# The up projection of an MLP by seven half-width products for each pair of blocks

## The chip, the cores and the metric

The kernel runs on one core of a Trainium2 chip. Its time is device microseconds of one execution; before the change the median of three runs is 988.55 us (988.21 to 988.84). The profile comes from one further execution.

## The reference

One decoder block on 512 tokens of 1,024 channels, in float32: a mixer (a state-space scan beside a pooling branch, merged by gates) and an MLP, each behind a normalisation with a scale and a shift from a conditioning vector. The change touches the MLP:

```python
h = rmsnorm(x, norm_mlp_w[i]) * (1.0 + scale_f) + shift_f
x = x + gate_f * (jnp.square(jax.nn.relu(h @ w_up[i])) @ w_down[i])
return rmsnorm(x, norm_final_w)
```

w_up is 1024 x 4096 and w_down 4096 x 1024.

## The kernel before

Channels lie on the 128 partitions, tokens along the free dimension. A weight matrix is cut into units: 128 output channels by 1,024 inputs, eight blocks of 128 x 128, one transfer of 512 KB (`load_unit`, from L125). Every float32 operand is split into a rounded high part and a low part: ScalarE writes the high part of a unit (L131), VectorE subtracts it for the low part (L132). A product of a block is three matmuls, high x high, high x low, low x high (`mm3`, L141 to L143), so a unit is 24 matmuls of 512 tokens into one PSUM bank. L111 and L112 split activations in the same way.

Raw units pass through four RAW buffers, split ones through four pairs of HL buffers, activations through 50 S buffers; `Slots` hands them out in turn, and a user waits for the last reader of the one before. A scheduler orders the instructions at build time within each engine's own queue, by the order in which the program is written and by priority; on the chip each queue runs in that order.

Behind the mixer comes `wout`: five whole units, then the last three in two halves of 256 tokens (`HALVES`), so that the norm of the first half runs beside the second. For each half, `residual` (L685, with the square L692 and its sum L693) makes x1, `norm` sums the squares on TensorE (L164), takes root and reciprocal (L176, L177) and spreads the result (L180), and `modulate` (L187 to L189) makes h2, the split input of the MLP.

The MLP runs in four quarters of the 4,096 hidden channels. A quarter has eight `up` units (Relu from PSUM, L739, square on VectorE, L731, split) and eight down units on the quarter's eight hidden tiles `us`, each added to x1 by `residual` (L685). The first three up units (`up_first`, Relu at L753) and the last three down units run in halves. The last quarter adds the sums of squares of the final norm, which ends in L781 and the writing of the output.

Of the kernel before, what the change touches and what calls it, by code (L numbers as in the profile page):

```python
# [18 lines left out]
HG = 8  # L19
# [14 lines left out]


NSLOT, NRAW, NHL, NPU = 50, 4, 8, 3
H = T // 2
# [21 lines left out]
def block_kernel(tc, xT, crow, arow, par, adaT, wstart, wz, wx, wpool_in, wgate, wpw, wbs, wbp, wout, wup, wdn, out):  # L59
    nc = tc.nc  # L60
    act, dve, pool, pe, sp = nc.scalar, nc.vector, nc.gpsimd, nc.tensor, nc.sync

    with (
# [3 lines left out]
    ):  # L67
        count = [0]

        def slots(name, n, shape=(P, T), where=sb):  # L70
            def make(i, dt):
                count[0] += 1
                return where.tile(list(shape), dt, tag=f"{name}{i}", name=f"{name}{i}_{count[0]}", bufs=1)
# [4 lines left out]
        MT = slots("mt", 3, (P, HG, P))  # L78
        RAW = slots("raw", NRAW, (P, 1024))
        HL = slots("hl", NHL, (P, 1024))  # L80
        SM = slots("sm", 4, (P, NC))
        SM.put(*[SM.get() for _ in range(4)])
        PU, PS = slots("ps", 8, (P, T), psp), slots("ps", 8, (P, T), psp)
        PU.free, PS.free = PU.free[:NPU], PS.free[NPU:]

        par_t = sb.tile([P, NPAR], F32, name="par_t")
# [5 lines left out]
        cbc = sb.tile([P, DM], F32, name="cbc")  # L92
# [15 lines left out]
        def split(src):  # L108

            hi, lo = S.get(F32R), S.get(F32R)  # L110
            act.copy(hi, src)  # L111
            dve.tensor_tensor(lo, src, hi.bitcast(F32), ALU.subtract)  # L112
            return hi, lo

        def free(pairs):
            for hi, lo in pairs:
                S.put(hi, lo)
# [3 lines left out]
        def load_unit(src, n=1024, low=None, at=None, cols=1024):  # L121

            at = at or HL
            with tc.high_priority() if urgent[0] else nullcontext():
                r = RAW.get()  # L125
                sp.dma_start(r[:, :n], src)
                blocks, kept = [], []
                for a in range(0, n, cols):
                    w = min(cols, n - a)
                    hi, lo = at.get(F32R), at.get(F32R)  # L130
                    act.copy(hi[:, :w], r[:, a:a + w])  # L131
                    (low or dve).tensor_tensor(lo[:, :w], r[:, a:a + w], hi[:, :w].bitcast(F32), ALU.subtract)  # L132
                    blocks += [(hi[:, o:o + P], lo[:, o:o + P]) for o in range(0, w, P)]
                    kept += [hi, lo]
            RAW.put(r)
            at.put(*kept)
            return blocks

        def mm3(ps, w, x, start, stop, t0=0, t1=T):
            (whi, wlo), (xhi, xlo) = w, x  # L140
            pe.matmul(ps, whi, xhi[:, t0:t1], start=start, stop=False)  # L141
            pe.matmul(ps, whi, xlo[:, t0:t1], start=False, stop=False)  # L142
            pe.matmul(ps, wlo, xhi[:, t0:t1], start=False, stop=stop)  # L143
# [29 lines left out]
        def rstd(sums, n, c0, c1):  # L173
# [6 lines left out]
                pe.matmul(bc[:, c * P:(c + 1) * P], r[:, c:c + 1].broadcast_to([P, P]), ident, start=True, stop=True)  # L180
            SM.put(r)
            return bc

        def modulate(x, R, scale, shift, hi, lo, t0=0, t1=T):

            t = S.get()
            dve.scalar_tensor_tensor(t[:, t0:t1], x[:, t0:t1], scale, R[:, t0:t1], ALU.mult, ALU.mult)  # L187
            act.activation(hi[:, t0:t1], t[:, t0:t1], AF.Identity, bias=shift)
            dve.scalar_tensor_tensor(  # L189
                lo[:, t0:t1], t[:, t0:t1], shift, hi[:, t0:t1].bitcast(F32), ALU.add, ALU.subtract)  # L190
            S.put(t)


        dve.memset(ones, 1.0)
# [15 lines left out]
        with tc.manual_schedule():  # L210
# [24 lines left out]
            ps = PU.get()  # L235
# [446 lines left out]
        def residual(ps, j, gate, t0=0, t1=T, sums=True, apart=None):  # L682

            x = x1[j][:, t0:t1]
            dve.scalar_tensor_tensor(x, ps[:, t0:t1], mod[:, gate + j:gate + j + 1], x, ALU.mult, ALU.add)  # L685
            if not sums:
                return
            if j == 0 or apart is not None:
                act.activation((ssum if apart is None else apart)[:, t0:t1], x, AF.Square)
            else:  # L690
                s = F.get()
                act.activation(s[:, t0:t1], x, AF.Square)  # L692
                dve.tensor_tensor(ssum[:, t0:t1], ssum[:, t0:t1], s[:, t0:t1], ALU.add)  # L693
                F.put(s)

        def norm(t0, t1, sqs):
            c0, c1 = t0 // P, t1 // P
            ps = PU.get()
            column_sums(ps, sqs, c0, c1)
            bc = rstd(ps, DM, c0, c1)  # L700
            PU.put(ps)
            return bc
# [8 lines left out]
                amod[:, 8 + k:9 + k], mod[:, 32 + k:33 + k], 1.0, col("nmlp", k), ALU.add, ALU.mult)  # L711
        w = [load_unit(wout[j], at=S, cols=T) for j in (5, 6, 7)]
        h2 = [(S.get(F32R), S.get(F32R)) for _ in range(8)]
        for t0, t1 in HALVES:
            for j in (5, 6, 7):
                ps = PU.get()
                for k in range(8):
                    mm3(ps[:, t0:t1], w[j - 5][k], mg[k], k == 0, k == 7, t0, t1)
                residual(ps, j, 16, t0, t1)
                PU.put(ps)  # L720
            R = norm(t0, t1, [ssum])
            for k in range(8):
                modulate(x1[k], R, amod[:, 8 + k:9 + k], mod[:, 24 + k:25 + k], *h2[k], t0, t1)
            PU.put(R)
        free(mg)
        for j in range(45, 48):
            ada(j)


        def squared(u):  # L730
            dve.tensor_tensor(u, u, u, ALU.mult)  # L731
            p = split(u)
            F.put(u)
            return p

        def up(i):
            ps = unit(wup[i], h2)
            u = F.get()
            act.activation(u, ps, AF.Relu)  # L739
            PU.put(ps)  # L740
            return squared(u)

        def up_first():

            w = [load_unit(wup[i]) for i in range(3)]
            u = [F.get() for _ in range(3)]
            for t0, t1 in HALVES:
                ps = [PU.get() for _ in range(3)]
                for k in range(8):
                    for i in range(3):  # L750
                        mm3(ps[i][:, t0:t1], w[i][k], h2[k], k == 0, k == 7, t0, t1)
                for i in range(3):
                    act.activation(u[i][:, t0:t1], ps[i][:, t0:t1], AF.Relu)  # L753
                PU.put(*ps)
            return [squared(t) for t in u]

        for q in range(4):
            us = up_first() if q == 0 else []
            us += [up(8 * q + i) for i in range(len(us), 8)]
            for j in range(8 if q < 3 else 5):  # L760
                ps = unit(wdn[4 * j + q], us)
                residual(ps, j, 40, sums=q == 3)
                PU.put(ps)
                if q == 3:
                    act.activation(x1[j], x1[j], AF.Copy, scale=col("nfin", j))
            if q < 3:
                free(us)
        w = [load_unit(wdn[4 * j + 3]) for j in (5, 6, 7)]
        last_sq = F.get()
        for t0, t1 in HALVES:  # L770
            for j in (5, 6, 7):
                ps = PU.get()
                for k in range(8):
                    mm3(ps[:, t0:t1], w[j - 5][k], us[k], k == 0, k == 7, t0, t1)
                residual(ps, j, 40, t0, t1, apart=last_sq if j == 7 else None)
                act.activation(x1[j][:, t0:t1], x1[j][:, t0:t1], AF.Copy, scale=col("nfin", j))
                PU.put(ps)
            R = norm(t0, t1, [ssum, last_sq])
            for j0, j1 in ((0, 2), (2, 4), (4, 6), (6, 8)):
                x = xbig[j0 // 4][:, j0 % 4:j0 % 4 + j1 - j0, t0:t1]  # L780
                dve.tensor_tensor(x, x, R[:, t0:t1].unsqueeze(1).broadcast_to([P, j1 - j0, t1 - t0]), ALU.mult)  # L781
                sp.dma_start(out[j0:j1, :, t0:t1].rearrange("j p t -> p j t"), x)
            PU.put(R)


# [69 lines left out]
```

## Time and profile before

| | us |
|---|---|
| median of three runs | 988.55 |
| the profiled execution | 988.34 |
| its span, first to last instruction | 986.6 |
| TensorE's clock granted in it, mean share of full speed | 0.997 |

A row of a group names line, engine, operation, tiles and shape, how often it ran, its busy us in total and the mean ns of one, and behind the second bar the idle time of its engine just before it with what ended it. In a timeline the first two numbers are the start in the span and the duration, both in us. PE is TensorE, PEld its weight loads, DVE is VectorE, ACT ScalarE, POOL GpSimd, SP the queue of ordinary transfers.

### The profile page before, as it was taken

The numbers are of one execution on the slowest core, as the hardware profiler recorded it, in microseconds if no ns is written. First come the engines' busy times: TensorE is split into PE (matmuls) and PEld (weight loads), VectorE is DVE, ScalarE is ACT, GpSimd is POOL, SyncE is SP. The second block draws the span as 40 slices with busy tenths as digits, with TensorE's granted clock in tenths as the row PEclk, the third lists the DMA queues.
The fourth block names the chain that finished last, engine by engine and source line by source line (L and its number), as shares of the span: only waits on it lengthen the run. The fifth ranks groups of instructions, "written<-read, shape, count | busy, mean of one in ns | idle before, by whom it ended". The sixth has DMA issues, their size and how long they took to land.

```text
span 986.6 us, 12153 instructions
## 1 busy us (share of the span) xinstructions
PE 971.5 (98%) x4722; PEld 802.3 (81%) x4722; DVE 616.0 (62%) x882; ACT 482.1 (49%) x719; POOL 63.8 (6%) x71
## 2 busy tenths in 40 slices
PE   8999999999999999999999999999999999999997
PEld 6777777888878878788888888988888888888886
DVE  6996967676776776878775665654344334434443
ACT  5488997579558833563312343452233123313342
POOL 0101120120012013200000000000000000000000
PEclk9999999999999999999999999999999999999998
DMA  9747342443343233337885443032232323232302
GB/s 349 278 131 205 106 139 89 125 119 108 103 134 115 86 124 112 123 112 237 269 273 186 166 147 129 2 128 91 101 97 96 106 87 107 86 107 86 107 1 86
DMA packets 58620, 129.55 MB, mean 131 GB/s; under 512 B 4609, under 2 KB 29313, under 8 KB 58562
## 3 DMA queue, kind: packets, MB, share of 16 engines
q1 hardware_dynamic: 58562, 128.77, 40.0%
q8 instruction: 37, 0.61, 0.3%
q14 instruction: 21, 0.17, 0.1%
HBM read 126.53 MB, written 2.23 MB: 130 GB/s over the span
## 4 chain that ended last, share of the span: by engine, by line
PE 82%; DVE 6%; ACT 5%; issue 4%; DMA 1%; POOL 1%; SPq 0%; DVEq 0%; POOLq 0%; ACTq 0%
PE ps L141 26%; PE ps L142 26%; PE ps L143 26%; PE ps L492 1%; DMA mt<-cs_d 1%; ACT hl L131 1%; DVE sz L157 1%; DVE hl L252 1%; ACT L359 1%; ACT mt L444 1%; ACT L444 1%; POOL pad L560 1%; PE ps L476 1%; PE ps L472 1%; DVE xs L157 1%
## 5 line engine op out<-in xcount | busy, mean ns | idle before, releaser
L141 PE MATMUL ps<-s,hl 128*128 128x512 f32 (+1 forms) x1272 | 490.3, 386 | 2.0 <-ACT pad L551 1.5
L142 PE MATMUL ps<-s,hl 128*128 128x512 f32 (+1 forms) x1272 | 485.7, 382 | 0.7 <-DVE s L112 0.7
L143 PE MATMUL ps<-s,hl 128*128 128x512 f32 (+1 forms) x1272 | 485.2, 382 | 0.0
L131 ACT CAST hl<-raw 128x1024 fp32r<-128x1024 f32 x153 | 160.0, 1048 | 287.9 <-PE ps L142 272.9
L141 PEld LDWEIGHTS ps<-s,hl 128*128 128x128 f32 x1272 | 239.2, 188 | 52.0 <-issue 3.5
L142 PEld LDWEIGHTS ps<-s,hl 128*128 128x128 f32 x1272 | 239.4, 188 | 47.1 <-DVE s L112 1.6
L143 PEld LDWEIGHTS ps<-s,hl 128*128 128x128 f32 x1272 | 239.2, 188 | 46.1
L132 DVE TENSOR_TENSOR hl<-raw,hl 128x1024 fp32r<-128x1024 f32 x153 | 188.3, 1233 | 126.7 <-ACT hl L131 123.6
L685 DVE SCALAR_TENSOR_TENSOR xs<-ps,mod,xs 128x512 f32<-128x512 f32 (+1 forms) x46 | 31.3, 681 | 106.3 <-PE ps L143 106.1
L111 ACT CAST s<-sz 128x512 fp32r<-128x512 f32 x52 | 31.6, 620 | 52.9 <-DVE sz L731 42.3
L157 DVE CUSTOM_DVE_ANT_0 raw<-raw,cbc,par_t 128x1024 f32<-128x1024 f32 x32 | 40.9, 1278 | 18.6 <-DMA raw<-adaT 18.3
L112 DVE TENSOR_TENSOR s<-sz,s 128x512 fp32r<-128x512 f32 x52 | 35.1, 689 | 22.7 <-ACT s L111 22.7
L444 ACT ACTIVATE mt<-mt,ncs 128x128 f32<-128x128 f32 x128 | 41.5, 392 | 13.6 <-POOL mt L440 13.4
L355 DVE SCALAR_TENSOR_TENSOR s<-ps,par_t,s 128x511 f32<-128x511 f32 (+2 forms) x54 | 40.2, 744 | 3.2 <-ACT s L353 2.8
L289 PE MATMUL ps<-s,hl 128*128 128x512 f32 x144 | 35.8, 399 | 0.7 <-ACT s L277 0.6
L289 PEld LDWEIGHTS ps<-s,hl 128*128 128x128 f32 x144 | 26.3, 188 | 8.9 <-ACT s L277 3.3
L359 ACT ACT_TABLE_LOAD x20 | 25.7, 1283 | 8.1 <-DVE s L355 7.8
L515 POOL TENSOR_TENSOR s<-s 128x256 f32<-128x256 f32 x16 | 17.2, 1073 | 154.1 <-ACT s L514 154.0
L440 POOL TENSOR_SCALAR_AFFINE_SELECT mt<-mt 128x1024 f32<-128x1024 f32 x16 | 19.1, 1191 | 121.4 <-ACT cd L437 81.3
L444 ACT ACT_TABLE_LOAD x19 | 24.4, 1283 | 0.3
L445 DVE TENSOR_TENSOR mt<-mt,ps 128x1024 f32<-128x1024 f32 x16 | 19.5, 1217 | 7.2 <-PE ps L427 3.6
L111 ACT CAST s<-s 128x512 fp32r<-128x512 f32 x16 | 9.9, 621 | 25.0 <-DVE s L564 24.7
(160 smaller groups left out, 760.8 us busy)
## 6 DMA issues: line engine op xcount, KB each, us to landing
raw<-adaT SPq DMA_DIRECT2D x32, 512.0 KB, 4.1
raw<-wup SPq DMA_DIRECT2D x32, 512.0 KB, 3.3
raw<-wdn SPq DMA_DIRECT2D x32, 512.0 KB, 3.2
raw<-wx SPq DMA_DIRECT2D x18, 512.0 KB, 3.7
raw<-wz SPq DMA_DIRECT2D x16, 512.0 KB, 3.3
mt<-cs_d SPq DMA_DIRECT2D x16, 512.0 KB, 5.9
raw<-wbs SPq DMA_DIRECT2D x16, 512.0 KB, 3.4
raw<-wgate SPq DMA_DIRECT2D x16, 512.0 KB, 4.0
```

The lines of the kernel that those rows point to most:

```text
L111: act.copy(hi, src)
L112: dve.tensor_tensor(lo, src, hi.bitcast(F32), ALU.subtract)
L131: act.copy(hi[:, :w], r[:, a:a + w])
L132: (low or dve).tensor_tensor(lo[:, :w], r[:, a:a + w], hi[:, :w].bitcast(F32), ALU.subtract)
L141: pe.matmul(ps, whi, xhi[:, t0:t1], start=start, stop=False)
L142: pe.matmul(ps, whi, xlo[:, t0:t1], start=False, stop=False)
L143: pe.matmul(ps, wlo, xhi[:, t0:t1], start=False, stop=stop)
L157: dve.tensor_tensor_reduce(r, r, cbc, 1.0, col("b_ada", j), ALU.mult, ALU.add, mod[:, j:j + 1])
L289: pe.matmul(first[u], w[u][i // 2], h[k][i % 2], start=k == 0 and i == 0, stop=k == 7 and i == 2)
L355: dve.scalar_tensor_tensor(t[:, sh:], ps[:, :T - sh], w(3 - sh), t[:, sh:], ALU.mult, ALU.add)
L359: act.activation(o, t, AF.Silu)
L444: act.activation(m[:, i, :], m[:, i, :], AF.Exp, bias=ncs[:, c, g * HG + i:g * HG + i + 1])
```

## The change

Two neighbouring up units are a pair. Its weights, a 2 x 2 arrangement of blocks (two groups of output channels A11, A12 and so on by even and odd input blocks), and its input, two token halves by even and odd blocks (B11 to B22), are multiplied in seven products of half the width instead of eight: `product` is 4 input blocks x 3 matmuls x 256 tokens, 12 matmuls. Both sides need sums. Of the input there are four, T1 to T4, made once behind the second norm (`sums`) from the unsplit tiles `hf`, which are kept for that. Of each pair's weights there are four, S1 to S4: two are begun by transfers on GpSimd's queue that add to what lies in the buffer, the rest VectorE adds (`prepare`).

The first two pairs of units run plainly as `up_first`, now four units in halves, since the sums aren't ready. The other 14 pairs are `Pair` jobs. A pair collects its result in two banks of a `duo` (c11, c12) and one bank `ac`; ScalarE copies one product to s5 and one to c11 between, and VectorE adds ac and s5. The Relu then reads both halves from two banks, and the square moves to ScalarE (`activated`). `run_jobs` writes the products of neighbouring pairs in turns. The down units stay plain, the first two of a quarter interleaved.

Around that: RAW, HL and the tiles of the scan share one set `d` of 16 buffers, which in the MLP becomes 8 raw and 10 split buffers, with four more of half size; two raw buffers lie in the `sz` tile that held the sums of squares until the second norm. The pooling branch has three pad buffers instead of six. Weights are laid out by `pairs`. The scratch for descriptors of GpSimd's transfers goes back to its default size.

```diff
+        duo = [psp.tile([P, 2, T], F32, name=f"duo{i}") for i in range(2)]
...
-        PADS = slots("pad", 6, (P, T + 16))
+        PADS = slots("pad", 3, (P, T + 16))
...
+        def sums(u1, u2, t1, t2):
+
+            dve.tensor_tensor(u1[:, :H], u1[:, :H], u1[:, H:], ALU.subtract)
+            dve.tensor_tensor(u1[:, H:], u2[:, H:], u1[:, H:], ALU.subtract)
+            dve.scalar_tensor_tensor(u2[:, H:], u2[:, H:], -1.0, u1[:, :H], ALU.mult, ALU.subtract)
+            dve.scalar_tensor_tensor(u2[:, :H], u2[:, H:], -1.0, u2[:, :H], ALU.mult, ALU.subtract)
+            two(u1, t1)
+            two(u2, t2)
...
+            with tc.high_priority():
+                y1, y2, y3, y4 = RAW.get(), RAW.get(), RAW.get(), Y4.get()
+                sp.dma_start(y1, w[:, :1024])
+                sp.dma_start(y3[:, T:], w[:, :T])
+                pool.dma_start(y1[:, :T], w[:, 3 * T:], accum_op=ALU.add)
+                pool.dma_start(y3[:, T:], w[:, T:2 * T], accum_op=ALU.add)
+                sp.dma_start(y2[:, T:], w[:, 2 * T:3 * T])
+                sp.dma_start(y4, w[:, 3 * T:])
+                s1, a11 = parts(y1)
+                dve.tensor_tensor(y2[:, :T], y1[:, :T], y1[:, T:], ALU.add)
+                RAW.put(y1)
+                s2, a12 = parts(y2)
+                dve.tensor_tensor(y3[:, :T], y2[:, :T], y2[:, T:], ALU.add)
...
+        def product(ps, a, b, start=False):
+            for m in range(4):
+                w = tuple(x[:, m * P:(m + 1) * P] for x in a)
+                for i, (x, y) in enumerate(((w[0], b[m][0]), (w[0], b[m][1]), (w[1], b[m][0]))):
+                    pe.matmul(ps, x, y, start=start and m == 0 and i == 0, stop=m == 3 and i == 2, skip_group_check=True)
...
+            def open(self):
+                self.be, self.s5 = BE.get(), U5.get()
+                self.c11, self.c12 = self.be[:, 0, :H], self.be[:, 1, :H]
+                product(self.c12, self.a["S1"], self.b["T1"], True)
+                act.copy(self.s5, self.c12)
+
+            def first(self):
+                self.ac = AC.get()
+                product(self.ac[:, :H], self.a["A11"], self.b["B11"], True)
+                act.copy(self.c11, self.ac[:, :H])
+
+            def middle(self):
+                product(self.ac[:, :H], self.a["S2"], self.b["T2"])
+                dve.tensor_tensor(self.c12, self.ac[:, :H], self.s5, ALU.add)
+                product(self.c11, self.a["A12"], self.b["B21"])
+
+            def third(self):
+                product(self.ac[:, :H], self.a["S3"], self.b["T3"])
+                dve.tensor_tensor(self.ac[:, H:], self.ac[:, :H], self.s5, ALU.add)
+                U5.put(self.s5)
+
+            def close(self):
+                product(self.c12, self.a["S4"], self.b["B22"])
+                self.done(0, self.be[:, :, :H], 1)
+                BE.put(self.be)
+                product(self.ac[:, :H], self.a["A22"], self.b["T4"])
+                self.done(1, self.ac.rearrange("p (a b) -> p a b", a=2), -1)
+                AC.put(self.ac)
...
+        def activated(q, p, i, ps, sign):
+
+            u = U.get()
+            act.activation(ab(u), ps, AF.Relu, scale=float(sign))
+            act.activation(u, u, AF.Square)
+            two(u, us[2 * p + i])
+            U.put(u)
...
+        def up_first(w):
+
+            ps = [PU.get(), PU.get(), AC.get(), AC.get()]
+            for t0, t1 in HALVES:
+                for k in range(8):
+                    for i in range(4):
+                        mm3(ps[i][:, t0:t1], w[i][k], h2[k], k == 0, k == 7, t0, t1)
+            for k in range(8):
+                act.activation(hf[k], hf[k], AF.Identity, bias=mod[:, 24 + k:25 + k])
+            for m in range(4):
+                sums(*hf[2 * m:2 * m + 2], *h2t[m])
...
+            for b in duo:
+                pe.matmul(b[:, 0, :], h2[0][0][:, :P], h2[0][0], start=True, stop=True)
+            for i in range(4):
+                activated(0, i // 2, i % 2, ab(ps[i]), 1)
```

How the build orders this is seen at three places. The first is VectorE's queue around the last residual ahead of the second norm (`xs` is x1, `sz` the squares, `sm` the norm's reciprocal). Before:

```order
L685 SCALAR_TENSOR_TENSOR xs_823_4716<-ps_897_5118,mod,xs_823_4716 128x256
L189 SCALAR_TENSOR_TENSOR s_879_4962<-s_894_5082,mod,s_878_4961 128x256
L189 SCALAR_TENSOR_TENSOR s_881_4964<-s_895_5086,mod,s_880_4963 128x256
L693 TENSOR_TENSOR sz_824_4717<-sz_824_4717 128x256
L685 SCALAR_TENSOR_TENSOR xs_823_4716<-ps_898_5146,mod,xs_823_4716 128x256
```

In the change (L763 is a low part: `d_850` and `d_855` are raw units of `up_first`, `d_825` the last quarter of a pair's weights; L687 the residual; L805 a weight sum into the buffer in the `sz` tile):

```order
L687 SCALAR_TENSOR_TENSOR xs_749_4643<-duo_68,mod,xs_749_4643 128x256
L733 SCALAR_TENSOR_TENSOR s_801_4885<-pad_810_4894,mod,s_800_4884 128x256
L733 SCALAR_TENSOR_TENSOR s_803_4887<-pad_811_4895,mod,s_802_4886 128x256
L763 TENSOR_TENSOR s_852_5173<-d_850_5170,s_851_5172 128x512
L763 TENSOR_TENSOR s_854_5177<-d_850_5170,s_853_5176 128x512
L763 TENSOR_TENSOR s_857_5183<-d_855_5180,s_856_5182 128x512
L763 TENSOR_TENSOR s_859_5187<-d_855_5180,s_858_5186 128x512
L763 TENSOR_TENSOR s_900_5536<-d_825_5139,s_899_5535 128x512
L687 SCALAR_TENSOR_TENSOR xs_749_4643<-duo_67,mod,xs_749_4643 128x256
L695 TENSOR_TENSOR sz_750_4644<-sz_750_4644 128x256 x3
L805 TENSOR_TENSOR sz_823_5137<-d_861_5191 128x512
L188 RECIPROCAL sm_818_5096<-sm_818_5096 128x2
```

Five low parts now stand ahead of the last residual, and a weight sum ahead of the norm's reciprocal.

The second place is the end of the sums on VectorE in the change (L768 to L770 are in `sums`, `pad` and `s_809` are `hf`, `s_840` and `s_842` high parts of T1 and T2; `d_893` and `d_895` high parts of weights of the second pair). Before, the three low parts of up units followed `modulate` here.

```order
L770 SCALAR_TENSOR_TENSOR s_809_4893<-s_809_4893 128x256
L767 TENSOR_TENSOR pad_810_4894<-pad_810_4894 128x256
L768 TENSOR_TENSOR pad_810_4894<-pad_811_4895,pad_810_4894 128x256
L763 TENSOR_TENSOR d_894_5522<-sz_823_5137,d_893_5521 128x1024
L763 TENSOR_TENSOR d_896_5527<-d_891_5513,d_895_5526 128x1024
L763 TENSOR_TENSOR s_839_5153<-s_809_4893,s_838_5152 128x512
L769 SCALAR_TENSOR_TENSOR pad_811_4895<-pad_811_4895,pad_810_4894 128x256
L763 TENSOR_TENSOR s_841_5155<-pad_810_4894,s_840_5154 128x512
L770 SCALAR_TENSOR_TENSOR pad_811_4895<-pad_811_4895 128x256
```

Two low parts of the next pair's weights came between the last block's sums.

The third place is ScalarE behind it, from the cast of the last `hf` to the copy of c11 (L916 Relu, L917 Square, L762 a cast, L834 the copy to s5, L839 the copy to c11; `ps_866` to `ps_869` are the four units of `up_first`, `ps_890` is the first pair's ac):

```order
L762 CAST s_842_5156<-pad_811_4895 128x512
L917 ACTIVATE pad_886_5466<-pad_886_5466 128x512
L834 COPY pad_827_5141<-duo_67 128x256
L762 CAST s_870_5448<-pad_886_5466 128x512
L916 ACTIVATE pad_887_5471<-ps_867_5213 128x512
L834 COPY pad_827_5141<-duo_68 128x256
...
L916 ACTIVATE pad_889_5481<-ps_869_5215 128x512
L917 ACTIVATE pad_889_5481<-pad_889_5481 128x512
L762 CAST d_897_5531<-d_892_5514 128x1024
L762 CAST s_876_5454<-pad_889_5481 128x512
L839 COPY duo_67<-ps_890_5499 128x256
```

The copy of the first pair's first product came to stand behind the activation of all four plain units. Before there was no such copy; three casts of weight units and three Relus stood here.

More of the change, by code (lines that the diff above doesn't have):

```diff
@@ L36 @@
 NSLOT, NRAW, NHL, NPU = 50, 4, 8, 3
+ND = 16
 H = T // 2
@@ L90, in col @@
             return par_t[:rows, a:a + n]
-        cbc = sb.tile([P, DM], F32, name="cbc")
+        cbc = slots("d", 1, (P, DM), first=NRAW + NHL + 3).get()
         ident = sb.tile([P, P], F32, name="ident")
@@ L713, in block_kernel @@
         h2 = [(S.get(F32R), S.get(F32R)) for _ in range(8)]
+        U = slots("pad", 2)
+        hf = [S.get() for _ in range(6)] + [U.get() for _ in range(2)]
         for t0, t1 in HALVES:
@@ L727, in block_kernel @@
             ada(j)
[L730 to L746, printed above, removed]
+        nmod = sb.tile([P, 8], F32, name="nmod")
@@ new lines, in block_kernel @@
+        dve.tensor_scalar(nmod, mod[:, 40:48], -1.0, None, ALU.mult)
+        for p_, t in zip((SZ, SZ), later):
+            p_.put(t)
+        raws, hls = SZ.get(), SZ.get(F32R)
+        D = lambda i, dt, n=1024: slots("d", 1, (P, n), first=i).get(dt)
+        RAW = Slots(lambda i, dt: D(i, dt) if i < 6 else raws[:, 2 * i - 12:2 * i - 10, :].rearrange("p a b -> p (a b)"), 8)
+        HL = Slots(lambda i, dt: D(i + 6, dt) if i < 8 else hls[:, 2 * i - 16:2 * i - 14, :].rearrange("p a b -> p (a b)"), 10)
@@ L755, in up_first @@
[L755 to L767, printed above, removed]
```

209 lines of the change are left out of this document (173 added, 36 removed).

## Prediction

> **What bounds the kernel now.** The page comes first: its span, its engines, its chain.
>
> ```profile
> span 986.6 us, 12153 instructions
> PE 971.5 (98%) x4722; PEld 802.3 (81%) x4722; DVE 616.0 (62%) x882; ACT 482.1 (49%) x719; POOL 63.8 (6%) x71
> PE 82%; DVE 6%; ACT 5%; issue 4%; DMA 1%; POOL 1%; SPq 0%; DVEq 0%; POOLq 0%; ACTq 0%
> ```
>
> TensorE is busy 98% of the span and holds 82% of the chain that ended last. A busy matmul row can hide waits, so the windows of the two stages that the change touches are next (length; then busy us of PE, PEld, DVE, ACT, POOL; granted clock; DMA share; GB/s).
>
> ```profile
> 606.00:644.00 38.00, 38.00 (x312) 37.54 (x311) 21.41 (x50) 15.43 (x32) 0.00 (x0) 1.00 0.05 16
> 644.00:980.00 336.00, 334.99 (x1559) 280.85 (x1558) 145.45 (x173) 108.77 (x147) 0.00 (x0) 1.00 0.28 91
> ```
>
> In the MLP (from 644) TensorE never rests, while VectorE works 145 of 336 us and ScalarE 109. So the time there is the number of matmuls times their spacing, and the side engines have room. The spacing is read from TensorE's timeline (start, duration), since durations overlap.
>
> ```profile
> 603.61 0.39 PE L141 MATMUL ps<-s,hl 128*128 128x512 f32 x1
> ...
> 606.11 0.39 PE L143 MATMUL ps<-s,hl 128*128 128x512 f32 x1
> 606.33 0.28 PE L141 MATMUL ps<-s,s 128*128 128x256 f32 x1
> ...
> 616.29 0.28 PE L143 MATMUL ps<-s,s 128*128 128x256 f32 x1
> ...
> 643.03 0.40 PE L141 MATMUL ps<-s,hl 128*128 128x512 f32 x1
> ```
>
> Twelve full-width starts lie 2.50/11 = 0.227 us apart, 84 half-width ones 9.96/83 = 0.120. Two halves therefore cost 0.240, 6% more than a whole. From 606.33 to 643.03 stand 288 half-width matmuls (34.56 us) and four small groups of the two norms, so 36.70 - 34.56 = 2.1 us for those; TensorE waits for nothing here.
>
> **The change part by part. TensorE's work.** A pair was 48 full-width matmuls, 48 x 0.227 = 10.9 us; it is now 84 half-width, 84 x 0.120 = 10.1. Over the program 694 full-width go (28 units of 24, the fourth first unit's 24, less 2 that open the duo banks), and 14 x 84 + 48 = 1,224 half-width come: -157.2 (at 0.2265, the 5.44 us of a unit over 24) + 146.9 = **-10.3 us**. The first four units in halves instead of three are in that count.
>
> **The side engines in the pair stages.** Durations (the mean ns behind the busy us):
>
> ```profile
> L131 ACT CAST hl<-raw 128x1024 fp32r<-128x1024 f32 x153 | 160.0, 1048 | 287.9 <-PE ps L142 272.9 <-issue 15.0
> L132 DVE TENSOR_TENSOR hl<-raw,hl 128x1024 fp32r<-128x1024 f32 x153 | 188.3, 1233 | 126.7 <-ACT hl L131 123.6
> L111 ACT CAST s<-sz 128x512 fp32r<-128x512 f32 x52 | 31.6, 620 | 52.9 <-DVE sz L731 42.3 <-DVE sz L659 8.5 <-DVE sz L534 2.0
> L112 DVE TENSOR_TENSOR s<-sz,s 128x512 fp32r<-128x512 f32 x52 | 35.1, 689 | 22.7 <-ACT s L111 22.7
> L739 ACT ACTIVATE sz<-ps 128x512 f32<-128x512 f32 x29 | 17.0, 585 | 0.0
> L692 ACT ACTIVATE sz<-xs 128x512 f32<-128x512 f32 x8 | 5.1, 632 | 4.0 <-DVE xs L685 4.0
> L753 ACT ACTIVATE sz<-ps 128x256 f32<-128x256 f32 x6 | 1.9, 375 | 0.1
> L693 DVE TENSOR_TENSOR sz<-sz,sz 128x256 f32<-128x256 f32 x5 | 2.1, 426 | 2.4 <-ACT sz L692 2.4
> L187 DVE SCALAR_TENSOR_TENSOR s<-xs,amod,ps 128x256 f32<-128x256 f32 x16 | 6.8, 476 | 0.8 <-PE ps L180 0.8
> ```
>
> ScalarE per pair: three whole casts and a half one (3.76), two copies of 256 (0.75), two Relu, Square and cast (3.67): 8.2 us. VectorE: three whole low parts and a half one (4.39), two weight sums (1.38), two PSUM sums of 256 (0.86), two low parts of the activations (1.38): 8.0. Both fit into the pair's 10.1 with 2 us to spare. In the orders of the later stages each handover has a product or two between (12 matmuls, 1.44 us, each): the copy of c11 is followed by 24 matmuls before the bank is needed, the sum into c12 by 17. Cost taken: nothing; TensorE's 10.1 hides it. With that cover gone each us too many is paid 12 times.
>
> **The junction: where cover is missing.** The second norm, the sums T1 to T4, four activations and the first two pairs meet here. VectorE's and ScalarE's timeline give their step when queued, shorter than a duration:
>
> ```profile
> 620.06 1.26 DVE L187 SCALAR_TENSOR_TENSOR s<-xs,amod,ps 128x256 f32<-128x256 f32 x3
> 627.08 0.48 DVE L685 SCALAR_TENSOR_TENSOR xs<-ps,mod,xs 128x256 f32<-128x256 f32 x1
> 629.80 0.17 DVE L177 RECIPROCAL sm<-sm 128x2 f32<-128x2 f32 x1 [1.26 <-ACT sm L176]
> 630.77 1.26 DVE L187 SCALAR_TENSOR_TENSOR s<-xs,amod,ps 128x256 f32<-128x256 f32 x3 [0.81 <-PE ps L180]
> 643.47 3.50 DVE L132 TENSOR_TENSOR hl<-raw,hl 128x1024 fp32r<-128x1024 f32 x3 [5.71 <-ACT hl L131]
> 646.89 1.89 DVE L731 TENSOR_TENSOR sz<-sz 128x512 f32<-128x512 f32 x3
> 642.39 2.95 ACT L131 CAST hl<-raw 128x1024 fp32r<-128x1024 f32 x3 [5.15 <-PE ps L142]
> ```
>
> Steps: VectorE 0.39 for a half scalar_tensor_tensor ((1.26 - 0.476)/2), 0.60 for 512, 1.13 for 1024, 0.34 for a half sum (0.426 less the same 0.085); ScalarE 0.95 for 1024 ((2.95 - 1.048)/2, 0.10 below its duration), so 0.52 cast, 0.49 Relu, 0.53 Square, 0.28 copy.
>
> *Second norm.* VectorE begins on the first half at about 620.3 as before: 16 operations and a residual, 17 x 0.39, to 627.0. Before, the last residual came then (627.08). Now five low parts of 512, each behind its cast, stand ahead of it (3.0, with the cast's lag 4.0), so it comes at 631.0; square and sum (0.9) bring 632.3. TensorE, with 192 half-width matmuls since 606.33 and half of the small groups, would be there at 630.4: a wait of about 2.1. VectorE restarts at 634.6 (629.80 to 630.77 for the broadcast, and one sum of 0.60 ahead of the reciprocal).
>
> *The sums.* Until T4's last part VectorE then has 24 half scalar_tensor_tensor (9.4), 8 half sums (2.7), seven low parts and two weight sums of 512 (5.4), three low parts of 1024 (3.4): 20.9, and 1.4 of waits for ScalarE in turn: 656.9. T1's last block is ready at 656.5; TensorE, done with the four units at 651.6, runs what it can and ends the two opening and two first products at 660.0, 2.7 later than its work alone.
>
> *The copy.* The next product, S2 x T2, adds into the bank that ScalarE must first copy to c11. On ScalarE that copy stands behind five casts (2.6), the first of which, of the last hf, waits until 656.9, four Squares (2.1), three Relus (1.5), two copies (0.6) and a cast of 1024 (0.95); with itself (0.38) that is 8.1, with four same-engine turnarounds of 0.1, 8.5. So TensorE goes on at 665.4; its work alone would have brought it there at 606.33 + 336 x 0.120 + 2.1 + 0.45 + 48 x 0.120 = 655.0. All waits of the junction: **+10.4 us**. Bounds: 5, if only norm and sums bind; 16, with late transfers (below). I take 10.4, since its queues are fixed and its steps are of these same operations. Afterwards the queues are level again within one pair.
>
> *The clock.* A rest of 5.4 us is longer than any that TensorE has here before its end (the longest, then windows).
>
> ```profile
> 12.58 0.59 PE L164 MATMUL ps<-ones,s 128*128 128x1 f32 x2 [2.82 <-DVE s L231]
> ```
>
> ```profile
> 10.00:12.00 2.00, 0.00 (x0) 0.00 (x0) 1.69 (x4) 1.93 (x3) 0.00 (x0) 1.00 1.03 421
> ...
> 981.00:982.00 1.00, 0.00 (x0) 0.00 (x0) 1.00 (x3) 0.00 (x0) 0.00 (x0) 0.64 0.00 0
> 982.00:983.00 1.00, 0.00 (x0) 0.00 (x0) 0.96 (x2) 0.00 (x0) 0.00 (x0) 0.50 0.91 304
> ```
>
> A rest of 2.82 us left the clock at 1.00; at the end it fell to 0.50, about 4 us after dense work stopped. Cost between 0 and half of the rest, 2.7. I take 1.2: half speed for as long as the rest goes beyond 3.0 us (2.4), costing half of that. [...]
>
> **Accumulating transfers** are not in this trace. The nearest rows (KB, us to landing):
>
> ```profile
> raw<-wup SPq DMA_DIRECT2D x32, 512.0 KB, 3.3
> xs<-xT SPq DMA_DIRECT2D x8, 256.0 KB, 4.6
> out<-xs SPq DMA_DIRECT2D x8, 256.0 KB, 2.7
> ```
>
> One of 256 KB takes 2.7 at best, and two passes of 4.6 (9.2) at worst. At 3.3, the value taken, they are hidden: pair 0's first is sent at 606.6, lands at 609.9, its addition at 613.2, when ScalarE wants it; that of the sz buffer, free only after the second norm, at about 640 where VectorE wants it at 639.2 (in the 1.4). [...] Later pairs are fetched some 20 us ahead, during the down units.
>
> **The rest.** Three pads instead of six: each copy into a pad stood already behind the split of the pooled tile before it on ScalarE, so nothing moves. Order shuffles in the scan stage: 0, bounds -1 and +1. Tail: same.
>
> **Sum.** 988.34 (span 986.6 and 1.7 around it) - 10.3 + 10.4 + 1.2 = 989.6; the median of the runs is 0.2 above the profiled execution: **989.8**.
>
> **The rivals.**
> 1. *The queues are shorter than counted*: only norm and sums delay (5.0), no long rest: 988.55 - 10.3 + 5.0 = 983.3. For it: my steps are sums of single rows; against: the order is fixed, and the copy is last. 0.22.
> 2. *Accumulated weights come late*, the one that ends well on the slow side. The first holds ScalarE and VectorE ahead of the first norm, that of the sz buffer ahead of the sums. It decides from 3.5 us per transfer; at 6.0 it adds 2.5 and 3.2: 995.5. For it: an addition must read what it adds to. Against: 2.7 for a plain one. 0.25.
> 3. *The pair stages don't hide their side work*: 80% load and waits in both directions, 0.5 us on each of 12 pairs: 996. Against: a product or two of slack at each handover. 0.10.
> 4. *Half-width products don't keep 0.120*, so the change doesn't do what it says: at 0.130, 1,176 of them cost 11.8: 1001. Against: 432 such matmuls run at 0.120 now. 0.03.
>
> The forecast, 987 to 992.5, has 0.40.
>
> **How the numbers follow.** Range 982.5 to 996: from rival 1's time to rival 3's; outside lie rival 4 and the far parts of 1 to 3, under 0.2. About 0.2% (2 us) can be told from no change. Faster than 986.6: rival 1 and a little of the forecast, 0.25. Within: most of the forecast up to 990.5, 0.27. Slower: its upper part and rivals 2 to 4, 0.48. The likeliest single time is still 989.8, inside the 0.2%.
>
> **What would show it.** Half-width starts 0.120 apart in the products; TensorE's waits listed with ScalarE's copy (some 5 to 6 us, once), VectorE's low parts (about 3) and the last residual's sum (about 2), nothing else over 1 in the MLP; the first down unit's end no earlier than before; a granted clock of 0.5 behind the long rest. The forecast is wrong if the copy's wait is short, if transfers lead the wait list, or if each pair shows a wait of its own.

## The result, and the profile after

The changed kernel takes 1031.1 us (median of four runs, 1027.2 to 1033.0) against 988.7: 1.0424 times as long, 95% interval 1.0408 to 1.0439. The forecast was 989.8, with a range up to 996.0. The profiled execution took 1032.95, its span 1031.2.

First the head of the page and its chain.

```profile
span 1031.2 us, 13636 instructions
PE 985.4 (96%) x5252; PEld 831.4 (81%) x5252; DVE 658.8 (64%) x961; ACT 537.0 (52%) x822; POOL 86.3 (8%) x99
PE 13%; DVE 1%; ACT 0%; DVEq 0%; issue 0%
```

The chain adds up to 14% of the span: followed back from the end it breaks off, so it names no cause, and the waits and windows have to. TensorE has 10.3 us less to do, yet is busy 13.9 us longer (985.4 against 971.5) and idle 30.7 longer (45.8 against 15.1). The two make up the 44.6 by which the span grew. So there are two things to look for, rests and slow work. For the rests there is TensorE's list of waits (in total, times, longest), here the rows of 0.8 and more that before did not have:

```profile
PE ps L821 <- DVE ps L848: 8.8, 3, 4.3
PE duo L152 <- DVE xs L650: 3.7, 1, 3.7
PE ps L821 <- ACT pad L916: 3.5, 1, 3.5
PE ps L153 <- DVE s L733: 3.4, 2, 3.1
PE ps L175 <- DVE sz L695: 2.8, 2, 2.6
PE duo L494 <- DVE d L447: 2.5, 1, 2.5
PE duo L450 <- ACT s L424: 2.3, 1, 2.3
PE duo L152 <- DVE xs L1002: 1.5, 1, 1.5
PE duo L821 <- DVE s L763: 0.8, 1, 0.8
```

ScalarE's copy, forecast to lead this list, is not in it. At the top stands VectorE's sum of ac and s5 (L848), in a pair stage that was counted as hidden. Four rows (L650, L447, L424, L1002) lie outside the stages that the prediction worked through; their matmuls write a `duo`. The slow work is in the windows (length; busy us of PE, PEld, DVE, ACT, POOL; granted clock; DMA share; GB/s):

```profile
620.00:640.00 20.00, 17.45 (x120) 17.05 (x119) 8.61 (x16) 6.22 (x11) 0.86 (x1) 0.85 0.32 86
680.00:700.00 20.00, 16.52 (x110) 15.74 (x111) 10.14 (x14) 14.67 (x27) 0.84 (x1) 0.83 0.35 104
940.00:960.00 20.00, 20.00 (x167) 19.73 (x166) 12.63 (x16) 14.55 (x24) 0.00 (x0) 1.00 0.50 168
```

Around rests the granted clock falls, to a mean of 0.85 and 0.83 in the first two rows. Over the span it is 0.981, before 0.997: with 1 and 0.5, the only values that the two traces hold, that is 39 us at half speed against 6, up to 16.6 us lost. With 10.3 us less to do and 13.9 more busy, 24.2 have to be found; the 7.6 that the clock leaves fit 19 more rests than before (29 against 10 in the full lists) at 0.4 each, an estimate from experiment 10, below. The last row is inside a series of pairs: TensorE without a rest at full clock, VectorE 63% and ScalarE 73% busy. There the prediction holds.

### The profile page after: what moved, and what is told of

The parts are those of the page before. It is cut to its first block, busy times and chain, and to the rows that moved or that the text cites. A ratio compares the mean times of both kernels' runs of the same rounds, so it can differ in the third digit from the quotient of the medians.

```text
span 1031.2 us, 13636 instructions
## 1 busy us (share of the span) xinstructions
PE 985.4 (96%) x5252; PEld 831.4 (81%) x5252; DVE 658.8 (64%) x961; ACT 537.0 (52%) x822; POOL 86.3 (8%) x99
## 5 line engine op out<-in xcount | busy, mean ns | idle before, releaser
L152 PE MATMUL ps<-s,d 128*128 128x512 f32 (+1 forms) x810 | 318.6, 393 | 3.1 <-ACT pad L553 1.5
L153 PE MATMUL ps<-s,d 128*128 128x512 f32 (+1 forms) x810 | 313.2, 387 | 3.9 <-DVE s L733 3.4
L154 PE MATMUL ps<-s,d 128*128 128x512 f32 (+1 forms) x810 | 311.8, 385 | 0.0
L152 PEld LDWEIGHTS ps<-s,d 128*128 128x128 f32 x810 | 153.2, 189 | 38.6 <-issue 3.7
L153 PEld LDWEIGHTS ps<-s,d 128*128 128x128 f32 x810 | 153.2, 189 | 35.9 <-DVE s L733 3.8
L154 PEld LDWEIGHTS ps<-s,d 128*128 128x128 f32 x810 | 153.1, 189 | 30.7 <-issue 0.4
L142 ACT CAST d<-d 128x1024 fp32r<-128x1024 f32 x89 | 92.8, 1044 | 117.8 <-PE ps L153 56.8
L143 DVE TENSOR_TENSOR d<-d,d 128x1024 fp32r<-128x1024 f32 x89 | 109.9, 1236 | 55.6 <-ACT d L142 53.7
L762 ACT CAST d<-d 128x1024 fp32r<-128x1024 f32 (+1 forms) x54 | 53.5, 993 | 105.5 <-PE ps L153 60.8
L763 DVE TENSOR_TENSOR d<-d,d 128x1024 fp32r<-128x1024 f32 (+1 forms) x54 | 62.0, 1153 | 35.5 <-ACT d L762 34.4
L821 PE MATMUL ps<-s,d 128*128 128x256 f32 x504 | 67.7, 289 | 3.5 <-ACT pad L916 3.5
L821 PEld LDWEIGHTS ps<-s,d 128*128 128x128 f32 x504 | 64.4, 197 | 4.3 <-ACT pad L916 3.7
L152 PE MATMUL duo<-s,d 128*128 128x512 f32 (+1 forms) x142 | 54.3, 385 | 5.2 <-DVE xs L650 3.7
L821 PE MATMUL duo<-s,d 128*128 128x256 f32 x420 | 57.1, 286 | 0.8 <-DVE s L763 0.8
L821 PEld LDWEIGHTS duo<-s,d 128*128 128x128 f32 x420 | 52.9, 191 | 3.9 <-DVE duo L843 1.6
L153 PE MATMUL duo<-s,d 128*128 128x512 f32 (+1 forms) x142 | 53.7, 378 | 0.0
L154 PE MATMUL duo<-s,d 128*128 128x512 f32 (+1 forms) x142 | 53.4, 377 | 0.0
L446 ACT ACTIVATE d<-d,ncs 128x128 f32<-128x128 f32 x128 | 41.6, 392 | 12.9 <-POOL d L442 12.6
L152 PEld LDWEIGHTS duo<-s,d 128*128 128x128 f32 x142 | 26.7, 188 | 12.7 <-DVE xs L650 4.4
```

Of the source, the lines that this page charges most:

```text
L446: act.activation(m[:, i, :], m[:, i, :], AF.Exp, bias=ncs[:, c, g * HG + i:g * HG + i + 1])
L762: act.copy(dst[0], src)
L763: dve.tensor_tensor(dst[1], src, dst[0].bitcast(F32), ALU.subtract)
L821: pe.matmul(ps, x, y, start=start and m == 0 and i == 0, stop=m == 3 and i == 2, skip_group_check=True)
```

## The experiments

Two suspects came from these lists: the PSUM tiles of two banks, and the accumulating transfers.

**Single banks.** TensorE's timeline in the gating stage, after, two rows that follow each other; then the row of VectorE's that ends the rest between them:

```profile
512.31 0.39 PE L152 MATMUL duo<-s,d 128*128 128x512 f32 x1
516.42 0.50 PE L152 MATMUL duo<-s,d 128*128 128x512 f32 x1 [3.73 <-DVE xs L650]
```

```profile
515.69 0.68 DVE L650 TENSOR_TENSOR xs<-xs,duo 128x512 f32<-128x512 f32 x1
```

A whole unit has been written into one half of a `duo`. The next goes into the other half, another bank, and starts at 516.42, when VectorE has read the first half (515.69 + 0.68). The order of the build shows that wait on the first matmul of the second unit:

```
L152 MATMUL duo_67<-s_541_3410,d_670_4113 128x512 [waits DVE_49]
```

With single banks the first matmul of such a unit waits for ScalarE's cast alone. Experiment 1 gives each bank its own tile:

```diff
-            if i >= 4:
-                return duo[(i - 4) // 2][:, i % 2, :]
...
-        BE = Slots(lambda i, dt: duo[i][:, :, :], 2)
+        be = [(bank(4 + 2 * i, F32), bank(5 + 2 * i, F32)) for i in range(2)]
+        BE = Slots(lambda i, dt: be[i], 2)
```

> The changed kernel with every PSUM bank a tile of its own: the two tiles of two banks (duo) go, c11 and c12 lie in two single banks, and the Relu that read both becomes two of 256. Theory (two banks in one tile make work on the one wait for work on the other): the extra 8.5 us of TensorE up to the pooling stage, the 3.7 wait for VectorE at 512 and the 1.5 at 1014 go, some 14 in all: 1017 (1013 to 1020), and the order of the scan is that of before. Rival (the merged buffers and the three pads cost the scan its time): no change, 1031.

Measured: 1014.5 (1012.9 to 1015.9), 16.6 less; ratio to before 1.0264 (1.0249 to 1.0279). One and the same matmul, the first that waits behind the pooling stage, in before, after and experiment 1:

```profile
406.23 0.51 PE L141 MATMUL ps<-s,hl 128*128 128x512 f32 x1 [1.54 <-ACT pad L551]
```

```profile
414.54 0.50 PE L152 MATMUL ps<-s,d 128*128 128x512 f32 x1 [1.50 <-ACT pad L553]
```

```profile
406.24 0.50 PE L148 MATMUL ps<-s,d 128*128 128x512 f32 x1 [1.50 <-ACT pad L549]
```

The 8.3 us lost by there are back to the hundredth, with merged buffers and three pads still in place: the rival falls. The order tells the same. Compared by operation, tiles and shape (without memsets, the merged buffers under one name), VectorE's first 633 instructions in the trace of experiment 1 stand in before's order; of the first 350 in the change's trace, 109 stand otherwise. Experiment 4 does this part alone, in the kernel before, with banks 6 and 7 as halves of one tile (the MLP is then kept to banks 0 to 3, off that tile):

```diff
-        PU, PS = slots("ps", 8, (P, T), psp), slots("ps", 8, (P, T), psp)
+        duo = [psp.tile([P, 2, T], F32, name=f"duo{i}") for i in range(1)]
+
+        def bank(i, dt):
+            if i >= 6:
+                return duo[0][:, i % 2, :]
+            count[0] += 1
+            return psp.tile([P, T], F32, tag=f"ps{i}", name=f"ps{i}_{count[0]}", bufs=1)
+
+        PU, PS = Slots(bank, 8), Slots(bank, 8)
```

> The kernel before with one edit: two of its eight PSUM banks are the halves of one tile. Theory of shared tiles: the scan's order changes and waits of 2 to 3 us appear in it, 3 to 10 us in all: 991.5 to 998.5. Rival (the tile's size means nothing): 988.5, no change beyond 0.5.

Measured: 1003.9 (1003.7 to 1004.1), 15.5 more; ratio 1.0157 (1.0142 to 1.0172). More than expected from one tile. Counted at equal work on TensorE, 12.6 of them are lost before the halves of `wout` (at 606.33 before), so ahead of the MLP and its smaller choice of banks. Its longest wait, in TensorE's list, is the same one as in the change:

```profile
PE duo L149 <- DVE xs L656: 6.4, 1, 6.4
```

**Weight sums on VectorE.** VectorE's timeline of the change at the head of three waits, then the queues that carry one of the transfers:

```profile
629.48 0.69 DVE L802 TENSOR_TENSOR d<-d 128x512 f32<-128x512 f32 x1 [2.04 <-DMA d<-wup]
...
662.97 0.69 DVE L802 TENSOR_TENSOR d<-sz 128x512 f32<-128x512 f32 x1 [4.21 <-DMA sz<-wup]
...
706.28 0.69 DVE L802 TENSOR_TENSOR d<-d 128x512 f32<-128x512 f32 x1 [4.40 <-DMA d<-wup]
706.89 1.22 DVE L763 TENSOR_TENSOR d<-d,d 128x1024 fp32r<-128x1024 f32 x1
708.03 0.69 DVE L805 TENSOR_TENSOR d<-d 128x512 f32<-128x512 f32 x1
708.63 0.42 DVE L848 TENSOR_TENSOR ps<-ps,pad 128x256 f32<-128x256 f32 x1
```

```profile
695.86 0.33 SPq L795 DMA_DIRECT2D d<-wup  x1
```

```profile
701.94 0.86 POOL L797 DMA_DIRECT2D d<-wup  x1 [5.86 <-DVE s L763]
```

The plain load goes out at 695.86, the transfer that adds to it at 701.94, and VectorE's weight sum starts at 706.28, when that has landed. The row puts GpSimd's wait down to VectorE, but the count of VectorE's that it asks for in the build's order is the one at which the plain load itself went out; besides, it waits there for that load, whose landing this trace doesn't hold. Two other such waits, which end at 625.24 and 712.54, are put down to the load itself. The sum stands in VectorE's queue ahead of L848, on which TensorE waits 4.3. This is the next quarter's pair, whose weights TensorE needs some 45 us later. The landings, in the list of transfers (KB, median us):

```profile
d<-wup SPq DMA_DIRECT2D x35, 256.0 KB, 3.8
d<-wup POOLq DMA_DIRECT2D x21, 256.0 KB, 4.7
sz<-wup POOLq DMA_DIRECT2D x7, 256.0 KB, 4.3
```

Experiment 2 lets VectorE make these two sums from what is loaded anyway; one plain load a pair goes as well, and the load of `y4` moves up:

```diff
-                sp.dma_start(y3[:, T:], w[:, :T])
-                pool.dma_start(y1[:, :T], w[:, 3 * T:], accum_op=ALU.add)
-                pool.dma_start(y3[:, T:], w[:, T:2 * T], accum_op=ALU.add)
...
+                dve.tensor_tensor(y3[:, T:], y1[:, :T], y1[:, T:], ALU.add)
+                dve.tensor_tensor(y1[:, :T], y1[:, :T], y4, ALU.add)
```

> The changed kernel without accumulating transfers: the two weight sums they made are two more additions of 128 x 512 on VectorE (1.2 us a pair) from pieces that are loaded anyway. Theory (VectorE's queue stands still behind a weight sum whose accumulated transfer has not landed): the waits of 2.55, 3.10, 4.35, 2.20 and 2.24 us on TensorE go or shrink below 1, some 12 to 15 and a few us of low clock with them: 1015 (1011 to 1020). Rival (the queue is late by its own work): 14 pairs get 1.2 us more each, none hidden at the series' ends: 1031 to 1036.

Measured: 1014.3 (1011.3 to 1014.9), 16.8 less; ratio 1.0252 (1.0235 to 1.0270). The waits for L848 are gone, and that at the first norm but for 0.3. That for L733 stays: in the change VectorE stood there for a transfer (at 662.97, above), here its own weight sums fill the time, and TensorE waits 3.3 instead of 3.1. In the series of pairs 1.2 us more of VectorE's work a pair costs nothing that shows. What is left of TensorE's list outside the `duo` rows:

```profile
PE ps L820 <- ACT pad L915: 3.8, 2, 1.9
PE ps L153 <- DVE s L733: 3.5, 2, 3.3
```

Experiment 3 makes both edits.

> Both edits: single banks and weight sums on VectorE. If the two causes are independent the gains add up: 1031 - 14 - 15 = 1002 (997 to 1006). If one hides the other (the same stretch of time is waited for twice) it is nearer 1010. What is left above 978 (before less the 10.3 of TensorE's work) is the junction of norm, sums and copy, estimated at 10 before the result.

Measured: 994.0 (993.1 to 997.6), 37.1 less than the change; ratio 1.0064 (1.0044 to 1.0083). The gains add up, and 3.7 more. Down to 0.6, its list names the junction and no other place that before's lacks:

```profile
PE ps L817 <- ACT pad L916: 3.9, 2, 2.0
PE ps L149 <- DVE s L729: 2.9, 1, 2.9
PE ps L148 <- ACT s L728: 1.0, 1, 1.0
PE ps L171 <- DVE sz L691: 0.9, 1, 0.9
```

Experiment 8 puts the accumulating transfers back into the best version (experiment 7, below):

> The kernel with single banks, plain pair and program order (984.3), with one thing put back: the two accumulating transfers of each pair instead of VectorE's two additions. Theory (a weight sum that waits for its accumulated transfer holds what VectorE has queued behind it, at the series' ends above all, whatever the junction does): waits of 2 to 4 us at three series' ends and about 1.5 of low clock at each: 994 (990 to 999). Rival (they were only late because the junction was): 984 to 986, or faster by VectorE's 1.2 us a pair.

Measured: 997.2 (992.5 to 997.8), 12.8 more than experiment 7; ratio 1.0074 (1.0056 to 1.0091). With nothing late at the junction, the series' ends wait again (the profiled execution, 992.8):

```profile
PE ps L822 <- DVE ps L844: 5.5, 2, 2.9
PE ps L822 <- DVE ps L849: 1.3, 1, 1.3
```

**The junction.** Three experiments on top of both edits. In the fifth the third pair runs as two whole plain units before the first products; in the sixth the first two pairs' weights are prepared in the order of the program; the seventh has the plain pair, and the first pair's weights in program order.

```diff
+        def up_plain(p):
+            def f(w):
+                ps = BE.get()
+                for k in range(8):
+                    for i in range(2):
+                        mm3(ps[i], w[i][k], h2[k], k == 0, k == 7)
+                for i in range(2):
+                    activated(0, p, i, ab(ps[i]), 1)
+                BE.put(ps)
...
-            with tc.high_priority():
+            with nullcontext() if len(calls) <= 1 else tc.high_priority():
...
-        ... up_first)] + [up(0, 2), up(0, 3)]
+        ... up_first)] + [up_plain(2), up(0, 3)]
```

> On top of both edits (994.0): the third pair of the first quarter also runs plainly, as two whole units between the first four units and the first products (48 full-width matmuls, 10.9 us, for 84 half-width ones, 10.1). Theory (the rest of the loss is the junction: ScalarE's and VectorE's queue there lack cover): the waits for ScalarE's Relu and copies (1.82 and 2.03) go, those ahead of the second half's products (0.97 and 2.85 for ScalarE and VectorE, with low clock behind them) stay unless the order moves: 994 + 0.8 - 4 to - 11, 988 (984 to 991). Rival (each pair costs time of its own, and the junction is not it): 994 + 0.8 = 995.

> On top of both edits (994.0): the first two pairs' weights are prepared in the order of the program instead of ahead of all that is ready, so that fewer weight sums and low parts stand among the second norm's work on VectorE; no unit is moved. Theory (queue order alone): the waits of 0.97 and 2.85 us ahead of the second half go, the same work is then late at the first products: 992 to 995. Rival (the order is the whole of the junction's loss): 984.

> Both of these on top of both edits: a plain pair as cover and the first pair's weights in program order. Theory: cover and order together leave the junction without a wait over 1 us; before less 10.3 plus 0.8 and 1 to 3 of small waits: 981 (979 to 985), faster than the kernel before. Rival (the junction's work on VectorE is too long for 11 us of cover): 986 to 990.

Measured: 984.9 (ratio 0.9964, 0.9951 to 0.9976), 991.4 (1.0033, 1.0020 to 1.0045) and 984.3 (0.9961, 0.9948 to 0.9975); experiment 6 lies just under its range. With 10.9 us of plain work between, the junction's waits go. The plain pair also spares VectorE and ScalarE one pair's sums and splits there; no run parts this from the cover that it gives. Order alone moves the waits: in experiment 6 TensorE waits where the products begin, for casts that now come late.

```profile
PE ps L821 <- ACT d L758: 3.4, 1, 3.4
PE ps L821 <- ACT s L758: 1.1, 1, 1.1
```

With the plain pair nothing over 0.7 is left in the junction, whatever the order. Experiment 7 is faster than before by 4.0 us (0.39%). Against experiment 5 it is the same.

**The clock.** Experiment 9 tried to shorten the rests at the series' ends in the kernel with single banks, by matmuls on a spare half bank ahead of the waiting product.

```diff
+                for _ in range(7):
+                    pe.matmul(self.be[0][:, H:H + P], ones, ones, start=False, stop=True, skip_group_check=True)
```

> The kernel with single banks (1014.5), and at each of the three series' ends seven matmuls of 128 x 128 on a spare half bank, 1.7 us, ahead of the product that waits there for VectorE (waits of 3.01, 2.95 and 2.81 in its trace, each with some 3 us of granted clock 0.5 behind it). The waits end when they did; only TensorE's rest is shorter, 1.1 to 1.3 us. Theory (a rest of that size leaves the clock at 1.00, one of 3 halves it): the stretches of 0.5 go, 1.3 to 1.6 us each: 1010 (1009 to 1012). Rival (the clock falls for another reason, or the slow stretch costs nothing since VectorE is late anyway): 1014.5, no change.

Measured: 1015.1 (1012.4 to 1017.6), no change. It did not do what it was for: at two of the three places the wait moved back with the added work and was as long as before (2.96 and 2.62); at the third it shrank to 1.53, and there the clock stayed at 1.00. So it decides nothing. Experiments 10 to 12 put rests into the kernel before, where TensorE never rests in the MLP: one, three or five additions of zero, in place, to the hidden block that ends one down unit and begins the next.

```diff
+                ks = range(8) if j % 2 == 0 else range(7, -1, -1)
...
+                if q < 3 and j < 3:
+                    for _ in range(3):
+                        dve.tensor_tensor(us[ks[7]][0], us[ks[7]][0].bitcast(F32), zero, ALU.add)
```

> The kernel before, with nine rests of TensorE put into the MLP on purpose: between the first four down units of three quarters VectorE adds zero to the block of hidden units that the one unit reads last and the next one first (one addition of 128 x 512, a rest of about 1.1 us by its step of 0.6 and the way there and back). Theory (a rest this short leaves the clock alone): 988.5 + 9 x 1.1 = 998.5 (996 to 1001), granted clock as before, 0.996 or more. Rival (every rest slows the clock): 1010.

> The same with three additions in a chain, rests of about 2.4 us (7 us more at none of the other waits). Theory (a rest of 1.8 to 3.5 us often, not always, brings some 3.4 us of clock 0.5 after or around it, 1.7 us lost): 988.5 + 9 x 2.4 = 1010, and 5 to 13 more: 1019 (1013 to 1026), clock 0.98 to 0.99. Rival (a rest costs its own length): 1010, clock 0.996.

> The same with five additions in a chain, rests of about 3.8 us. Theory: nearly every rest brings a stretch of clock 0.5, of which part lies in the rest itself: 988.5 + 9 x 3.8 = 1023, and 7 to 15 more: 1033 (1028 to 1040). Rival: 1023, clock 0.996.

Measured: 995.5 (ratio 1.0071, 1.0054 to 1.0088), 1026.7 (1.0383, 1.0368 to 1.0399), 1035.9 (1.0478, 1.0463 to 1.0494). Only six of the nine places rested, and three additions made a longer rest than estimated, as each list says (total, times, longest):

```profile
PE ps L141 <- DVE s L770: 4.7, 6, 0.8
```

```profile
PE ps L141 <- DVE s L770: 23.4, 6, 3.9
```

```profile
PE ps L141 <- DVE s L770: 32.1, 6, 5.4
```

The spans are 993.9, 1023.0 and 1034.1, so 7.3, 36.4 and 47.5 over before's 986.6. In the first the clock never falls in the MLP, and the 2.6 beyond the rests' 4.7 is 0.4 for each rest. The second has 36.4 - 23.4 - 2.6 = 10.4 left, 1.7 a rest, the third 12.8, 2.1 a rest: the clock. Windows of experiment 11 in a rest, behind it, and after that:

```profile
687.30:691.00 3.70, 0.00 (x0) 0.00 (x0) 3.67 (x5) 0.84 (x1) 0.00 (x0) 1.00 0.09 12
691.30:694.30 3.00, 3.00 (x8) 2.35 (x9) 0.00 (x0) 0.00 (x0) 0.00 (x0) 0.52 0.35 141
694.70:698.00 3.30, 3.30 (x16) 2.75 (x15) 0.00 (x0) 0.00 (x0) 0.00 (x0) 0.98 0.00 0
```

Eight full-width matmuls in 3 us at 0.52, sixteen in 3.3 at 0.98. A rest of 3.9 costs itself, 0.4, and 1.7: the theory, not the rival.

## Why the prediction was wrong, step by step

**TensorE's work, -10.3: right.** Products start 1.44 us apart, 0.120 a matmul, also with PSUM tiles in turns:

```profile
753.94 1.59 PE L821 MATMUL duo<-s,d 128*128 128x256 f32 x12
755.37 1.60 PE L821 MATMUL ps<-s,d 128*128 128x256 f32 x12
```

The fourth rival falls with it.

**"Order shuffles in the scan stage: 0" and "Tail: same": wrong, the first failed step.** The PSUM tiles were taken for a matter of names. Two banks in one tile made a write to the one wait for a read of the other (3.73 us to 516.42), and the build's order bent around that. Counted at equal work on TensorE, the change is 8.3 us behind at the pooling stage and 13.7 at the halves of `wout` (3.7 of the difference is the rest in gating), experiment 1 only 0.2; a rest of 1.5 in the tail comes on top. Undoing it gives 16.6, doing it alone costs 15.5. The bounds of -1 and +1 had no row behind them, and no rival named the tiles.

**Accumulating transfers "at 3.3, hidden", pairs "fetched some 20 us ahead": wrong, the second failed step.** The mechanism was the second rival's, at 6.0 us a transfer: 2.5 us at the first norm and 3.2 before the sums. TensorE waited 2.55 and 3.10 there. That the numbers meet is partly luck: a transfer lands 4.3 to 4.7 after it is sent, and the second wait stays without any (3.3 in experiment 2), so it isn't shown to be the transfers'. What makes them late is that each is sent only behind the plain load below it: from the first load to the weight sum 10.4 us passed at 706.28. The rival also left out a third place, and the largest. With high priority the next pairs' sums stand far ahead in VectorE's queue, so at each series' end L848 waits behind a transfer that nobody else needs yet, 8.8 us in three places. Taking the transfers out gave 16.8 us with the clock they cost. The case was named and given 0.25; its price was too low by its third place and by the clock.

**The junction, 10.4 and 1.2: about right in size, in part for other reasons, so in part by luck.** Experiment 3 has what is left with both edits: 994.0 against 988.5 - 10.3 = 978.2, so 15.8 for 11.6. The queues named, five low parts and ScalarE's activations of the four plain units, do bind. But the first products wait for ScalarE's Relu of a plain unit, in whose bank ac lies (3.5 in the change, 3.9 in experiment 3), before the copy of c11 can matter; the copy was the wrong instruction of the right queue. And the second half's modulated blocks, not counted, come 2.9 late behind the second pair's weight sums. In experiment 5, which puts 10.9 us of plain work for 10.1 of products, 9.1 us are gained, so 9.9 of the 15.8 go; the other 5.9 are in no wait of the junction over 0.7, and no run here takes them apart. (The wait at the second norm is 2.1 in the prediction's text, 1.9 by its own times, and 2.4 in what its sum adds up to; this changes nothing here.)

**The clock, half speed "beyond 3.0 us": wrong, the third failed step.** The row that it rests on, a rest of 2.82 us at 1.00, was misread: TensorE ran at half speed before and after that rest. Before's trace has no record of the clock ahead of 18.72 us, and what isn't recorded counts as 1.00. The norm's small matmuls show it in the trace itself, first at the start and then in the last quarter:

```profile
15.73 1.91 PE L180 MATMUL ps<-ident,sm 128*128 128x128 f32 x8
970.23 0.60 PE L180 MATMUL ps<-ident,sm 128*128 128x128 f32 x4
```

Within the first row they start 0.213 us apart, within the second 0.111. Experiment 7's record holds the start; the same stretch in before and in it:

```profile
12.50:17.50 5.00, 4.92 (x23) 4.92 (x24) 2.59 (x6) 1.36 (x3) 0.00 (x0) 1.00 1.03 417
12.50:17.50 5.00, 4.91 (x23) 4.91 (x24) 2.60 (x6) 1.36 (x3) 0.00 (x0) 0.50 1.03 415
```

So that row could bound nothing, and no run shows the 3.0. In the change rests of 2.20 to 2.55 each brought half speed, up to 16.6 us in all against 1.2 forecast.

**Pair stages hidden: right** inside a series, as the window at 940 shows. The third rival's 0.5 us a pair did not come; with 1.2 us a pair more on VectorE (experiment 2) it still did not.

Together: 989.8 forecast and 1031.1 measured are 41.3 apart; 37.1 go with the two edits (experiment 3): 16.6 and 16.8, each with the clock that its rests cost, and 3.7 that only both together give. The 4.2 left are 15.8 less the 11.6 that the prediction gave to the junction.

## What to carry to other kernels

When a change touches how PSUM banks are grouped into tiles, follow every user of those tiles, also in stages that the change is not about. A transfer that feeds an instruction in a busy engine's queue holds what stands behind it, as L848 here, 8.8 us in three places; ask what that is, above all where the order has pulled it ahead of its need. A saving on the bound engine needs cover for what it starts: here one pair left plain, 0.8 us more on TensorE, was worth 9. And a rest of the bound engine can cost more than its length: at 3.9 us, in experiment 11, it cost 0.4 and 1.7 besides.

## What the runs showed of the hardware

In the change's trace the records of the granted clock begin at 19.7 us. From there on TensorE's timeline has nine rests of 2.20 to 4.35 us, and half clock came at eight of them, from 2.3 us before the end of the rest (to 684.18) to 1.2 behind it (to 796.76): six stretches of 3.41 us and two of 6.83. Two rests of 1.50 brought none, nor did the six of up to 0.8 in experiment 10. Each rest of experiment 11 brought 3.41 us at 0.5 (one of the six 6.83), each of experiment 12 brought 6.83, of which 1.7 to 3.1 lay in the rest. The length alone doesn't tell: the ninth rest in the change, of 3.73 (to 516.42), left the clock at 1.00, and one of 2.20 (to 796.76) brought half clock (busy TensorE is the first number behind the length, the clock the third from the end):

```profile
512.50:516.40 3.90, 0.19 (x1) 0.00 (x0) 3.34 (x7) 0.15 (x1) 0.00 (x0) 1.00 0.82 259
516.40:520.00 3.60, 3.58 (x16) 2.96 (x17) 2.39 (x3) 0.00 (x0) 0.00 (x0) 1.00 0.86 304
```

```profile
793.00:797.00 4.00, 1.80 (x16) 1.60 (x15) 4.00 (x7) 1.54 (x2) 0.00 (x0) 1.00 0.44 76
797.00:800.00 3.00, 3.00 (x16) 2.71 (x16) 1.52 (x2) 1.42 (x3) 0.00 (x0) 0.66 0.70 210
```

What parts the two, and what brings full clock back, is left open here. Runs of one kernel differ by the clock: the six of experiment 8 lie at 992.5 and 992.8 with a mean clock of 0.996, and at 996.8 to 997.8 with 0.986 to 0.992.

An accumulating transfer of 256 KB landed after 4.3 to 4.7 us by the medians, a plain one of that size after 2.9 in experiment 2 and 3.8 in the change.
